# A hybrid attention and convolution layer: two latents, a row norm and the positions by other routes, the first weights in halves, one output quarter by TensorE

## The chip, the cores and the metric

The kernel runs on one core of a Trainium2 chip. The metric is the device time of one execution in microseconds (us). Five engines work side by side, each through its own list in order: TensorE (PE) multiplies matrices, VectorE (DVE) and ScalarE (ACT) work element by element, GpSimd (POOL) does small work and issues transfers, SyncE (SP) issues transfers.

## The reference, cut to what matters

x is 256 rows of 2048; w_in has 2048 x 15,424 weights; there are 16 heads.

```python
h = _rmsnorm(x, pre_norm_g)
proj = jnp.einsum('bsd,de->bse', h, w_in)
(q_a, c_kv, k_rope, z_mla, c_in, b_gate, c_gate, z_conv,
 g_mla, g_conv) = jnp.split(proj, cuts, axis=-1)
q = jnp.einsum('bsr,re->bse', _rmsnorm(q_a, q_a_norm_g), w_q_b)
...
kv = jnp.einsum('bsr,re->bse', _rmsnorm(c_kv, kv_a_norm_g), w_kv_b)
...
q_rope = _apply_rope(q_rope, cos[:, :, None, :], sin[:, :, None, :])
k_rope = _apply_rope(k_rope, cos, sin)
attn = _causal_mla_attention(q_nope, q_rope, k_nope, k_rope, v)
attn = attn.reshape(b, s, MLA_WIDTH) * jax.nn.silu(z_mla)
y_mla = jnp.einsum('bse,ed->bsd', attn, w_o_mla)
...
merged = jax.nn.sigmoid(g_mla) * y_mla + jax.nn.sigmoid(g_conv) * y_conv
out = jnp.einsum('bsd,de->bse', merged, w_out)
x = x + _rmsnorm(out, post_norm_g)
```

q_a and c_kv, the two latents, are 512 wide each; k_rope is 64 wide. cos and sin come from the positions. The row norm of x scales every row of proj.

## The kernel before, in words

**Products in two halves.** Every float32 operand is split into a rounded high half (ScalarE, line 237) and the rest (VectorE, line 238), and a product is three TensorE products: high by high, high by low, low by high. Weights come in units of 128 x 2048 values over SP's queue (load_raw, line 150), are split in halves of 1024 columns (split_unit) and are used in the order of a list, plan, that is written out by hand (lines 113 to 145). take(i) loads some units ahead and splits one ahead. There are three raw buffers, and five buffers each for the high and low halves; units 3, 4 and 5 land in areas of tiles that are not yet in use.

**Order.** Most instructions are placed by a scheduler, which takes what is ready, earlier lines first. keep_in_program_order holds a marked instruction behind those marked before it on its engine; all of TensorE's instructions are marked (lines 86 to 91).

**Start.** x comes transposed, in row blocks k of 128 features by 256 rows. The first eight units hold two such blocks each and the two matching blocks of q_a's weights. Block 0 of x comes with the small parameters (pv, line 247) on ScalarE's queue. Unit 0 comes in two pieces, units 1 and 2 in two each (line 155). Each block is scaled by pre_norm_g and split into x_both (split_scaled, line 334): block 0 is scaled by VectorE, the others by ScalarE, and VectorE makes all the low halves. Nine idle products (line 265) run on TensorE ahead of it. latent_products (line 456) accumulates q_a, with the 256 rows as two tiles; then c_kv (four units) and k_rope (u_kr) follow.

**Positions.** tables() (line 392) computes the angles on GpSimd, in a long row of small operations behind four transfers of the positions, each to 32 partitions, from GpSimd's own queue (line 396). Two sines on ScalarE follow, 32 copies into cos_t and sin_t on GpSimd (line 439) and a sign on VectorE (line 442). It is a generator: each next(table_parts) issues the part up to the next yield.

**Norms and turns.** The row norm of x is computed from x_tok: squares on ScalarE, a power on GpSimd (inverse_root, line 356), r_col by rows. input_rows (line 374) makes r_x, the same numbers along a row in every partition, by two TensorE products of ones by a diagonal (rb). latent_norm (line 465) scales a latent by rows out of PSUM into lat_f; latent_turn (line 477) transposes it with TensorE, eight transposes of 128 x 128 for each latent (lt_qa, lt_ckv), and ScalarE and VectorE make the halves, qa and ckv, from PSUM. q_a is turned after the first unit of z, c_kv in the middle of the second one (turn_keys, line 769).

**Another way to turn** stands in turned() (line 308), which the gates, the probabilities and the channels use: VectorE transposes blocks of 32 x 32 into a tile (line 312), GpSimd's queue stores it to DRAM in four transfers (go, line 319), and one load brings it back (come, line 323). A load waits for its four stores.

**First head.** z (four units) gives the gates of four heads, closed by gates_done (line 668). Then make(...) computes from qa and ckv the first group: q and k without rotation for two heads ("a": qn, kn), the rotated part of q ("r": qr, rotated by VectorE in rope, line 446) and the values ("v": vv); then a quarter of the convolution channels, channels(0, 0) (cv), and the scores of head 0 (sc, scores, line 582). sc needs qn, kn, qr and the rotated key kr (key_rope, line 523). From there, channels, scores and values alternate over 16 heads; then the wide products (sq) and the last one (out).

**End.** out_block (line 950) sums the squares of a block of 512 columns on ScalarE and multiplies by post_norm_g on VectorE. Behind the last block of a row tile, row_norm (line 961) gives rr, and finish (line 968) makes og * rr + xr on VectorE in five pieces, each stored from SP's queue.

Of the kernel before, what the change touches and what calls it, by code (L numbers as in the profile page):

```python
# [82 lines left out]
def tile_layer(ctx: ExitStack, tc: tile.TileContext, xw, x, pos, pvec, post_g, wc, wz, wcv, wkr, wqk, wqr, wv, cwr, wsq, out):  # L83
# [6 lines left out]
    def transpose(*a):  # L90
        return tc.keep_in_program_order(nc.tensor.transpose(*a))  # L91

# [69 lines left out]
    def split_unit(i):  # L162
# [84 lines left out]
    nc.scalar.dma_start(out=pv[:, :], in_=pvec)  # L247
    x_first = pv[:, -(-PV_N // LINE) * LINE :]
# [16 lines left out]
    for _ in range(9):  # L265
# [5 lines left out]
    r_both = const.tile([P, LINE], F32, name="r_both")  # L271
    r_col, r_sq = r_both[:, :NT], r_both[:, NT : 2 * NT]
# [35 lines left out]
    def turned(src, via, n):  # L308
# [4 lines left out]
        far = dram.tile([P, P * n], F32, name="far", tag=f"far{n}", bufs=4)  # L313

        def go():
            f = far[:, :].rearrange("(q y) (i m) -> i y q m", q=4, i=4)
# [4 lines left out]
        def come(dst):  # L321

            tc.keep_in_program_order(nc.gpsimd.dma_start(out=dst, in_=far[:, :]))
# [10 lines left out]
    def split_scaled(dst, src, k):  # L334
        if k == 0:
            a = nc.vector.tensor_scalar(dst[:, k, :S], src, col("pre_g", k), None, op0=ALU.mult)
        else:
            a = nc.scalar.activation(dst[:, k, :S], src, AF.Copy, scale=col("pre_g", k))
        tc.keep_in_program_order(a)
# [21 lines left out]
    def input_norm():  # L361
# [5 lines left out]
        dgs = []  # L367
        for t in range(NT):
            dg = temp(f"dg{t}", (P, P), tag=f"rms_d{t}", bufs=1)
            nc.vector.tensor_scalar(dg[:, :], ident[:, :], r_col[:, t : t + 1], None, op0=ALU.mult)  # L370
            dgs.append(dg)
        return dgs

    def input_rows(dgs):

        rb = bank("rb", tag="st", bufs=1)
        for t in range(NT):
            matmul(rb[:, t * P : (t + 1) * P], ones[:, :], dgs[t][:, :], start=True, stop=True)
        nc.scalar.activation(r_x[:, :], rb[:, :S], AF.Copy)
# [11 lines left out]

    def tables():

        pi = temp("ta_i", (P, SQ), I32, 1)
        for q in range(4):
            nc.gpsimd.dma_start(
                out=pi[32 * q : 32 * q + 32, :], in_=pos[:, SQ * q : SQ * (q + 1)].to_broadcast([32, SQ])
            )
# [36 lines left out]
        for o in range(4):  # L435
            for q in range(4):
                to, ti = slice(32 * o, 32 * o + 32), slice(32 * q, 32 * q + 32)
                for dst, src in ((cos_t, n1), (sin_t, n2)):
                    tc.keep_in_program_order(nc.gpsimd.tensor_copy(dst[to, SQ * q : SQ * (q + 1)], src[ti, :]))
        yield  # L440
# [15 lines left out]
    def latent_products(pss, k, w, wk):  # L456
        cols = [x_both[:, k, o : o + P] for o in (0, P, S, S + P)]
        wh, wl_ = w(wk, R)
        for i, ws, first, last in ((0, wh, True, False), (2, wh, False, False), (0, wl_, False, True)):
            for t in range(NT):  # L460
                matmul(
                    pss[t][:, :], cols[i + t], ws, start=first and k == 0, stop=last and k == KD - 1
                )

    def latent_norm(name, pss):
# [11 lines left out]
    def latent_turn(name, both, g, tags):  # L477
        f = lat_f[name]
        for j2 in range(2):
            ps = bank(f"lt_{name}{j2}", tag=tags[j2][0], bufs=tags[j2][1])  # L480
            for j in range(2):
                for t in range(NT):
                    o, b = j * S + t * P, 2 * j2 + j
                    transpose(ps[:, o : o + P], f[:, t, b * P : (b + 1) * P], ident[:, :])
            for j in range(2):
                b, src = 2 * j2 + j, ps[:, j * S : (j + 1) * S]
                nc.scalar.activation(both[:, b, :S], src, AF.Copy, scale=col(g, b))
                nc.vector.scalar_tensor_tensor(
                    both[:, b, S:], src, col(g, b), both[:, b, :S].bitcast(F32), op0=ALU.mult, op1=ALU.subtract
                )  # L490

    table_parts = tables()
    next(table_parts)
    ps_q = [bank(f"qa{t}") for t in range(NT)]
    for i in range(KD // 2):
        ahead(u_qa[i], raw=3 + len(early), split=0)
        w = take(u_qa[i])
        for j in range(2):
            latent_products(ps_q, 2 * i + j, w, j)
    ps_c = [bank(f"ckv{t}") for t in range(NT)]  # L500
    for i in range(4):
# [3 lines left out]
        if i == 0:  # L505
            next(table_parts)
        if i == 1:
            dg = input_norm()
            latent_norm("qa", ps_q)
# [6 lines left out]
    input_rows(dg)  # L516
    latent_norm("ckv", ps_c)
# [16 lines left out]
    def narrow(names, w, j, src, **kw):  # L534
        pss = [bank(n, **kw) for n in names]
# [117 lines left out]
    def quarter(pss, w, i, between=None):  # L653

        for t in range(NT):
            if t and between:
                between()
# [5 lines left out]
    def gates(v, i, between=None):  # L663
        if i == 0:
            z_ps["now"] = [bank(f"z{v}_{t}") for t in range(NT)]
        quarter(z_ps["now"], take(u_gate[v][i]), i, between)
# [95 lines left out]
    for h in range(H):  # L762
        v, at = divmod(h, HV)

        if at == 0:
            for i in range(4):
                if v == 0 and i == 1:

                    def turn_keys():
                        latent_turn("ckv", ckv, "kv_g", (("mm", 4), ("mm", 4)))  # L770
                        next(table_parts)

                    gates(v, i, turn_keys)
                else:
                    gates(v, i)
                if v == 0 and i == 0:
                    latent_turn("qa", qa, "q_g", (("st", 1), ("o", 1)))
                elif v == 0 and i == 2:
                    key_rope()
# [187 lines left out]

    def finish(t, rr):
        for a, b in ((0, 256), (256, 512), (512, 1024), (1024, 1536), (1536, 2048)):
# [18 lines left out]
    for t in range(NT):  # L988
# [4 lines left out]
        finish(t, out_block(3, t, pss[t]))  # L993
# [90 lines left out]
```

## Time and profile before

| | us |
|---|---|
| median of 3 runs | 1038.44 (1038.15 to 1038.61) |
| the profiled execution | 1039.19 |
| its span, first to last instruction | 1037.4 |
| TensorE busy in it | 1027.2 |

TensorE's granted clock was 0.998 of full speed. In the profile's rows "L88" is a line of the kernel; PE is TensorE's products and PEld its loading of weights; a row of the chain has a start, a length, an engine, a tile and a count. Tiles have the names that the code gives them, without numbers: qa, ckv, kr, rb, z, lt_qa, qn, kn, qr, vv, cv, sc, sq and out are banks of PSUM that TensorE writes.

### The profile page before, as it was taken

What the parts mean: (1) busy time and instruction counts of PE and PEld (TensorE: products, weight loads), DVE (VectorE), ACT (ScalarE), POOL (GpSimd) and SP (SyncE); (2) the same over time, 40 slices, a digit from 0 to 9 for tenths busy, and PEclk for the clock granted to TensorE, in tenths of its full rate; (3) what the DMA queues carried; (4) which work ended last, traced back from release to release, by engine and by line L of the source; (5) the groups of instructions that cost most, each with busy time, mean ns of one, the idle gap of its engine ahead of it and who ended that gap; (6) DMA issues with size and microseconds to landing.
All of it is one profiled execution on the core that took longest, in us unless ns stands there. A gap on an engine that the chain in (4) does not pass through costs nothing.

```text
span 1037.4 us, 12723 instructions
## 1 busy us (share of the span) xinstructions
PE 1027.2 (99%) x4694; PEld 856.3 (83%) x4694; DVE 682.3 (66%) x954; ACT 526.6 (51%) x733; POOL 181.0 (17%) x345
## 2 busy tenths in 40 slices
PE   9999999999999999999999999999999999999996
PEld 7888888888888888888888888888888888888885
DVE  7579777787687786767777785564465455455562
ACT  7767555555555455554554564444334434443551
POOL 7620321114211232212313120020010001002000
PEclk9999999999999999999999999999999999999999
DMA  8745766568565685757676766565555566558642
GB/s 323 304 175 215 232 213 234 193 222 295 190 250 202 219 282 189 272 210 243 236 262 200 261 228 212 183 228 198 203 203 209 197 203 236 181 191 331 235 165 82
DMA packets 41952, 231.04 MB, mean 223 GB/s; under 512 B 7521, under 2 KB 8225, under 8 KB 18977
## 3 DMA queue, kind: packets, MB, share of 16 engines
q1 hardware_dynamic: 29808, 197.54, 53.9%
q0 software_dynamic: 11648, 29.38, 8.5%
q10 hardware_dynamic: 432, 3.29, 0.8%
q8 instruction: 37, 0.61, 0.2%
q14 instruction: 27, 0.21, 0.1%
HBM read 214.48 MB, written 11.53 MB: 218 GB/s over the span
## 4 chain that ended last, share of the span: by engine, by line
PE 98%; DMA 1%; DVE 0%; ACT 0%; SPq 0%; DVEq 0%; issue 0%
PE cv L88 34%; PE sq L88 34%; PE z L88 8%; PE out L88 8%; PE qn L88 2%; PE kn L88 2%; PE vv L88 2%; PE ckv L88 2%; PE qa L88 2%; PE sc L88 1%; PE qr L88 1%; PE o L88 1%; DMA raw<-xw_dram 1%; PE kr L88 0%; DVE og L971 0%; PE lt_qa L91 0%
## 5 line engine op out<-in xcount | busy, mean ns | idle before, releaser
L238 DVE TENSOR_TENSOR wlo<-raw,whi 128x1024 fp32r<-128x1024 f32 (+1 forms) x370 | 441.1, 1198 | 284.1 <-ACT whi L237 273.9
L237 ACT ACTIVATE whi<-raw 128x1024 fp32r<-128x1024 f32 (+1 forms) x372 | 382.9, 1035 | 396.2 <-PE sq L88 180.5
L88 PE MATMUL cv<-whi,x_both 128*128 128x512 f32 x1024 | 321.1, 389 | 0.0
L88 PEld LDWEIGHTS cv<-whi,x_both 128*128 128x128 f32 x1024 | 192.3, 188 | 39.2
L88 PE MATMUL cv<-wlo,x_both 128*128 128x512 f32 x512 | 199.5, 390 | 0.0
L88 PE MATMUL sq<-whi,x_both 128*128 128x512 f32 x512 | 158.3, 389 | 0.0
L88 PEld LDWEIGHTS sq<-whi,x_both 128*128 128x128 f32 x512 | 96.1, 188 | 19.9
L88 PEld LDWEIGHTS cv<-wlo,x_both 128*128 128x128 f32 x512 | 96.2, 188 | 19.0
L88 PE MATMUL sq<-wlo,x_both 128*128 128x512 f32 x256 | 99.6, 389 | 0.0
L88 PE MATMUL z<-whi,x_both 128*128 128x512 f32 x256 | 80.6, 390 | 0.0
L88 PE MATMUL sq<-whi,at_both 128*128 128x512 f32 x256 | 79.5, 389 | 0.0
L88 PE MATMUL sq<-whi,cv_both 128*128 128x512 f32 x256 | 79.4, 389 | 0.0
L88 PE MATMUL out<-whi,m_both 128*128 128x512 f32 x256 | 78.9, 389 | 0.0
L319 POOL DMA_DIRECT2D far<-sg x32 | 17.5, 555 | 312.2 <-DVE sg L312 238.6
L319 POOL DMA_DIRECT2D far<-via x64 | 35.4, 560 | 195.1 <-DVE via L312 194.7
L88 PEld LDWEIGHTS sq<-wlo,x_both 128*128 128x128 f32 x256 | 48.0, 188 | 10.0
L88 PEld LDWEIGHTS z<-whi,x_both 128*128 128x128 f32 x256 | 48.1, 188 | 9.9
L88 PEld LDWEIGHTS sq<-whi,at_both 128*128 128x128 f32 x256 | 48.0, 188 | 9.9
L88 PEld LDWEIGHTS out<-whi,m_both 128*128 128x128 f32 x256 | 48.0, 188 | 9.9
L88 PEld LDWEIGHTS sq<-whi,cv_both 128*128 128x128 f32 x256 | 48.0, 188 | 9.9
L88 PE MATMUL z<-wlo,x_both 128*128 128x512 f32 x128 | 49.8, 389 | 0.0
L88 PE MATMUL sq<-wlo,at_both 128*128 128x512 f32 x128 | 49.8, 389 | 0.0
(214 smaller groups left out, 1128.0 us busy)
## 6 DMA issues: line engine op xcount, KB each, us to landing
raw<-wsq_dram SPq DMA_DIRECT2D x80, 1024.0 KB, 4.7
raw<-wcv_dram SPq DMA_DIRECT2D x64, 1024.0 KB, 5.8
raw<-wz_dram SPq DMA_DIRECT2D x16, 1024.0 KB, 4.7
raw<-wqk_dram SPq DMA_DIRECT2D x8, 1024.0 KB, 5.1
cw<-cwr_dram POOLq DMA_DIRECT2D x24, 256.0 KB, 6.2
raw<-wc_dram SPq DMA_DIRECT2D x4, 1024.0 KB, 9.9
raw<-wv_dram SPq DMA_DIRECT2D x4, 1024.0 KB, 4.7
far<-via POOLq DMA_DIRECT2D x64, 48.0 KB, 3.3
```

The costliest lines, as they stand in the source:

```text
L88: return tc.keep_in_program_order(nc.tensor.matmul(*a, **kw))
L237: a = nc.scalar.activation(hi, src, AF.Copy)
L238: b = nc.vector.tensor_tensor(lo, src, hi.bitcast(F32), op=ALU.subtract)
L319: tc.keep_in_program_order(nc.gpsimd.dma_start(out=f[i], in_=m))
```

## The change

- **Latents.** latent_norm now turns the scaled latent itself: VectorE transposes 32 x 32 blocks of each row tile, GpSimd's queue stores them (eight stores for each latent), and it hands back one load (qa_come, ckv_come). latent_split makes the halves from SBUF. TensorE's sixteen transposes go, and latent_turn and the between of quarter with them.
- **Row norm.** r_x comes by a VectorE transpose of a 128 x 32 tile, two stores and one broadcast load on GpSimd's queue. rb, its diagonals and input_rows go.
- **Positions.** The host hands them over as 128 rows; one transfer on SP's queue, behind the sixth unit, brings them. The parts of tables() are issued at other places, the copies in two parts.
- **Start.** Block 0 of x, unit 0's first weights and their splits come in halves; block 0's products too; VectorE scales block 1 as well; seven idle products for nine.
- **Order.** channels(0, 0) runs ahead of the first group, in the plan too; key_rope comes behind "a"; qr's products of the first group use the common banks.
- **End.** For the second row tile, columns 0 to 511 of the result are x by the identity plus og by a diagonal of rr on TensorE (identity product ahead of the norm), copied and stored by ScalarE; VectorE does the other 1536 in four pieces. The first row tile has four pieces.

```diff
-        order += (first if h == 0 else []) + [(h, 0), (h, 1), (h, 2)] + made[h] + [(h, 3)]
+        order += [(h, 0)] + (first if h == 0 else []) + [(h, 1), (h, 2)] + made[h] + [(h, 3)]
...
-        cuts = {0: (S, XW, 2 * XW), 1: (0, XW, 2 * XW), 2: (0, XW, 2 * XW)}.get(i, (0, w))
+        cuts = {0: (S, 2 * S, XW, 2 * XW), 1: (0, XW, 2 * XW), 2: (0, XW, 2 * XW)}.get(i, (0, w))
...
+        if i == u_qa[5]:
+            tc.keep_in_program_order(nc.sync.dma_start(out=tables_pi, in_=pos))
...
-                split_act(hi[:, j * R : (j + 1) * R], lo[:, j * R : (j + 1) * R], t[:, o + S : o + XW], True)
+                for a, b in ((0, S), (S, R)) if k == 0 else ((0, R),):
+                    cs = slice(j * R + a, j * R + b)
+                    split_act(hi[:, cs], lo[:, cs], t[:, o + S + a : o + S + b], True)
...
-    nc.scalar.dma_start(out=pv[:, :], in_=pvec)
+    for a, b in ((0, n + P), (n + P, n + S)):
+        nc.scalar.dma_start(out=pv[:, a:b], in_=pvec[:, a:b])
...
-    for _ in range(9):
+    for _ in range(7):
...
-        if k == 0:
-            a = nc.vector.tensor_scalar(dst[:, k, :S], src, col("pre_g", k), None, op0=ALU.mult)
+        if k < 2:
+
+            for a, b in ((0, P), (P, S)) if k == 0 else ((0, S),):
+                tc.keep_in_program_order(
+                    nc.vector.tensor_scalar(dst[:, k, a:b], src[:, a:b], col("pre_g", k), None, op0=ALU.mult)
+                )
...
+        rt = temp("r_turned", (P, LINE), bufs=1)
+        temp("pad_n", (P, S - LINE), bufs=1)
+        nc.vector.transpose(rt[:, :], r_both[:, :])
+        far = dram.tile([NT, S // NT], F32, name="far_r")
+        rows_of = rt[:, :].rearrange("(q y) x -> y q x", q=4)
+        for t in range(NT):
+            tc.keep_in_program_order(
+                nc.gpsimd.dma_start(out=far[t, :].rearrange("(q x) -> q x", q=4), in_=rows_of[t])
+            )
+        return lambda: tc.keep_in_program_order(
+            nc.gpsimd.dma_start(out=r_x[:, :], in_=far[:, :].rearrange("t s -> (t s)").unsqueeze(0).to_broadcast([P, S]))
+        )
...
+            for a, b in ((0, S), (S, R)) if halved else ((0, R),):
+                for t in range(NT):
+                    matmul(
+                        pss[t][:, a:b], cols[i + t], ws[:, a:b], start=first and k + a == 0, stop=last and k == KD - 1
+                    )
...
         inverse_root(r[:, :], v[:, :])
+        if then:
+            then()
         nc.vector.tensor_tensor(r[:, :], r[:, :], r_col[:, :], op=ALU.mult)
+        far = dram.tile([P, NT * R], F32, name=f"far_{name}")
         for t in range(NT):
             nc.scalar.activation(f[:, t, :], pss[t][:, :], AF.Copy, scale=r[:, t : t + 1])
+            go, _ = turned(f[:, t, :], temp("cw", (P, 512), bufs=2), 4, far[:, t * R : (t + 1) * R])
+            go()
+        return lambda: tc.keep_in_program_order(
+            nc.gpsimd.dma_start(out=f, in_=far[:, :].rearrange("p (t c) -> p t c", t=NT))
+        )
+
+    def latent_split(name, both, g):
+
+        f = lat_f[name].rearrange("p t (i k x) -> p k t i x", i=4, k=KR)
+        for k in range(KR):
+            hi, lo = (both[:, k, o : o + S].rearrange("p (t i x) -> p t i x", t=NT, i=4) for o in (0, S))
+            tc.keep_in_program_order(nc.scalar.activation(hi, f[:, k], AF.Copy, scale=col(g, k)))
+            tc.keep_in_program_order(
+                nc.vector.scalar_tensor_tensor(lo, f[:, k], col(g, k), hi.bitcast(F32), op0=ALU.mult, op1=ALU.subtract)
+            )
...
-    input_rows(dg)
-    latent_norm("ckv", ps_c)
+    r_come()
+    ckv_come = latent_norm("ckv", ps_c, qa_come)
+    next(table_parts)
+    ckv_come()
+    next(table_parts)
...
-        kw = {} if g else {"tag": "cv", "bufs": 2}
-        (f,) = narrow([f"qr{g}"], take(u_grp["r", g]), 0, qa, **kw)
+        (f,) = narrow([f"qr{g}"], take(u_grp["r", g]), 0, qa)
...
+                gates(v, i)
+                if v == 0 and i == 2:
+                    latent_split("qa", qa, "q_g")
...
+            else:
+                latent_split("ckv", ckv, "kv_g")
             gates_done(v)
         if h == 0:
+            channels(h, 0)
             for i in first:
                 make(*i)
-            channels(h, 0)
+                if i[0] == "a":
+                    next(table_parts)
+                    key_rope()
...
+    def ahead_of_norm(t):
+
+        fin = bank("fin", tag="st", bufs=1)
+        matmul(fin[:, :], ident[:, :], xr[:, t, :512], start=True, stop=False)
+        return fin
+
+    def by_tensor(t, rr, fin):
+
+        dg = op.tile([P, P], F32, name="dg_fin")
+        tc.keep_in_program_order(nc.scalar.activation(dg[:, :], ident[:, :], AF.Copy, scale=rr[:, 0:1]))
+        matmul(fin[:, :], dg[:, :], og[:, t, :512], start=False, stop=True)
+        o = op.tile([P, 512], F32, name="o_fin")
+        tc.keep_in_program_order(nc.scalar.activation(o[:, :], fin[:, :], AF.Copy))
+        nc.scalar.dma_start(out=out[t * P : (t + 1) * P, :512], in_=o[:, :])
+
     def finish(t, rr):
-        for a, b in ((0, 256), (256, 512), (512, 1024), (1024, 1536), (1536, 2048)):
+        cuts = ((0, 512), (512, 1024), (1024, 1536), (1536, 2048))
+        if t:
+            cuts = ((512, 768), (768, 1024), *cuts[2:])
```

More of the change, by code (lines that the diff above doesn't have):

```diff
@@ L271, in tile_layer @@
     r_both = const.tile([P, LINE], F32, name="r_both")
+    nc.gpsimd.memset(r_both[:, :], 0.0)
     r_col, r_sq = r_both[:, :NT], r_both[:, NT : 2 * NT]
@@ L305, in temp, with turned @@
         return bp.tile([P, -(-n // LINE) * LINE], dt, name=name, tag=tag, bufs=bufs)[:, :n]
-    def turned(src, via, n):
+    def turned(src, via, n, far=None):
         via = via[:, : P * n]
@@ L321, in come @@
         def come(dst):
-            tc.keep_in_program_order(nc.gpsimd.dma_start(out=dst, in_=far[:, :]))
+            tc.keep_in_program_order(nc.gpsimd.dma_start(out=dst, in_=far))
         return go, come
@@ L389, in rows @@
         nc.vector.tensor_tensor(dst, dst, r_x[:, :], op=ALU.mult)
+    tables_pi = temp("ta_i", (P, SQ), I32, 1)
     def tables():
[L394 to L398, printed above, removed]
+        pi = tables_pi
         y, n1, n2, r = (temp(f"ta_{n}", (P, SQ), bufs=1) for n in "ymnr")
@@ L453, in rope, with latent_products @@
         nc.vector.tensor_tensor(dst, a[:, :], b[:, :], op=ALU.add)
-    def latent_products(pss, k, w, wk):
+    def latent_products(pss, k, w, wk, halved=False):
         cols = [x_both[:, k, o : o + P] for o in (0, P, S, S + P)]
@@ L459, in latent_products, with latent_norm @@
         for i, ws, first, last in ((0, wh, True, False), (2, wh, False, False), (0, wl_, False, True)):
[L460 to L465, printed above, removed]
+            for a, b in ((0, S), (S, R)) if halved else ((0, R),):
[3 more added lines that the diff above has]
+                    )
+    def latent_norm(name, pss, then=None):
         f = lat_f[name]
@@ L532, in tile_layer, with narrow @@
     groups = {}
-    def narrow(names, w, j, src, **kw):
-        pss = [bank(n, **kw) for n in names]
+    def narrow(names, w, j, src):
+        pss = [bank(n) for n in names]
         halves([
@@ L651, in tile_layer, with quarter @@
     z_ps = {}
-    def quarter(pss, w, i, between=None):
+    def quarter(pss, w, i):
         for t in range(NT):
-            if t and between:
-                between()
             for k4 in range(4):
@@ L661, in quarter, with gates @@
                 product(pss[t][:, :], a, w(k4, 512), k == 0, k == KD - 1)
-    def gates(v, i, between=None):
+    def gates(v, i):
         if i == 0:
             z_ps["now"] = [bank(f"z{v}_{t}") for t in range(NT)]
-        quarter(z_ps["now"], take(u_gate[v][i]), i, between)
+        quarter(z_ps["now"], take(u_gate[v][i]), i)
     def gates_done(v):
@@ L992, in tile_layer @@
             out_product(pss[t], t, last[kk], kk)
-        finish(t, out_block(3, t, pss[t]))
+        fin = ahead_of_norm(t) if t else None
+        rr = out_block(3, t, pss[t])
+        if t:
+            by_tensor(t, rr, fin)
+        finish(t, rr)
 def _cols(w):
```

65 lines of the change are left out of this document (16 added, 49 removed).

## The prediction

> **What bounds the kernel now.** I read the shares of the engines first, then who TensorE (PE) waited for, then the chain of work that ended last, in order of time.
>
> ```profile
> PE 1027.2 (99%) x4694; PEld 856.3 (83%) x4694; DVE 682.3 (66%) x954; ACT 526.6 (51%) x733; POOL 181.0 (17%) x345
> ```
>
> ```profile
> PE qa L88 <- ACT whi L237: 1.2, 1, 1.2
> ```
>
> ```profile
> 1.64 6.58 DMA raw<-xw_dram
> ...
> 9.33 19.38 PE qa L88 x84
> ...
> 50.47 3.63 PE kr L88 x16
> 54.09 0.45 PE rb L88 x4
> 54.54 5.46 PE z L88 x24
> 60.00 0.87 PE lt_qa L91 x8
> 60.87 2.75 PE z L88 x12
> 63.62 0.87 PE lt_ckv L91 x8
> 64.49 13.64 PE z L88 x60
> 78.13 2.77 PE qn L88 x16
> 80.90 2.79 PE kn L88 x16
> 83.69 1.40 PE qr L88 x8
> 85.09 5.49 PE vv L88 x24
> 90.58 5.44 PE cv L88 x24
> 96.02 0.94 PE sc L88 x8
> ```
>
> The first number of a chain row is the start, the second the length, in us. TensorE is the bound: 99% busy, and behind its wait of 1.2 us, which ends at 9.33, its products follow one another to the end. So an edit counts in one of four ways: products taken out of TensorE's stream, the start of that stream, a new wait inside it, and the tail after it. What it does to the other engines costs nothing until TensorE waits for them.
>
> **The change part by part.** The profiled execution took 1039.19 us (span 1037.4 and 1.8 around it); the median of the three runs shown is 1038.44, 0.75 less. I sum differences, and apply them to both.
>
> *Products taken out.* The row norm's four instructions (rb, 0.45) and the sixteen transposes of the two latents (0.87 each) stand in the chain itself: 0.45 + 0.87 + 0.87 = **2.19 us** gone. Added there is nothing of that size: the first row block's 6 products become 12 of half the width, and the identity product of the last quarter follows TensorE's last product, in the tail.
>
> *The start.* TensorE's first real products come well before 9.33:
>
> ```profile
> 5.00 1.23 PE L88 MATMUL qa<-whi,x_both 128*128 128x512 f32 x4
> ```
>
> At the z products' pace (13.64/60 = 0.227 us) the 12 products of the first two row blocks take 2.7 us from 5.0, to 7.7; then TensorE stands until 9.33, since the third block's rows land at 1.64 + 6.58 = 8.2 and ScalarE needs 1.1 us more. Why so late? I looked at the DMA view of the first 5 us, and at stretches around it (the last column is GB/s, the one before the share of the DMA engines):
>
> ```profile
> DMA packets 508, 1.03 MB, mean 207 GB/s; under 512 B 49, under 2 KB 177, under 8 KB 508
> ```
>
> ```profile
> 5.00:8.00 3.00, 3.00 (x14) 2.17 (x13) 1.96 (x4) 1.03 (x2) 0.00 (x0) 1.00 0.88 290
> 8.00:20.00 12.00, 10.76 (x48) 8.81 (x48) 10.80 (x21) 10.96 (x24) 8.97 (x14) 1.00 1.03 429
> ```
>
> ```profile
> q0 software_dynamic: 102, 0.03, 6.5%
> ```
>
> Up to and with those rows 144 + 256 + 384 + 384 KB (by the tiles' shapes) = 1.20 MB are queued; by 5.0 us 1.03 MB had moved, so 0.17 MB were left, some 0.5 us at either stretch's rate. The rows were not whole until 8.2, and just between 5 and 8 the traffic drops from 429 to 290 GB/s. The last row is that stretch's GpSimd queue: 102 packets, of the four transfers of positions (line 396). The change takes these away: positions come on SP's queue, behind the sixth unit. So I expect the rows at some 6.2 to 6.6, ScalarE done by 7.7, and TensorE in the third block at 7.7 instead of 9.33: **1.65 us** saved. Its bounds: 0, if something else holds one DMA engine back, and 2.3, if the halved loads also bring the first two blocks 0.65 forward. I take 1.65 since the second block needs its own transfer and VectorE's chain, now one scaling longer (the scaled rows of block 1 move there from ScalarE). Two more issues, SP's and ScalarE's, stand before these rows; what matters here is queued bytes, which stay the same. Two idle products fewer only end the warm-up before the earlier start.
>
> *GpSimd's side of the positions.* On SP's queue the seventh unit's load stands behind them, and that one waits for a free buffer anyway. They land behind the sixth unit, so the angle arithmetic starts about 6.5 us later; there is a hole ahead of the row norm's power that takes it:
>
> ```profile
> 40.73 0.73 POOL L358 TENSOR_TENSOR r_both<-v_x,mhalf 128x2 f32<-128x2 f32 x1 [7.06 <-DVE v_x L364]
> ```
>
> *The latents through DRAM.* This adds four VectorE transposes, 16 stores and 2 loads on GpSimd's queue, plus 2 stores and 1 load for the row norm; 32 table copies stand around them. Their nearest rows are the gates' and probabilities' trips and the copies:
>
> ```profile
> L319 POOL DMA_DIRECT2D far<-via x28: 548/554/657, 101.8 to 287.1; - x28
> ...
> DMA to landing us min/median/max: 1.9/4.0/7.1
> ```
>
> ```profile
> L439 POOL COPY cos_t<-ta_m 32x64 f32<-32x64 f32 x16 | 8.4, 524 | 0.6
> ```
>
> The c_kv products end at 50.47 - 1.65 = 48.8. GpSimd's queue from there is, at worst in series: 8 stores of q_a (8 x 0.55 = 4.4), their landing (4.0) that q_a's load waits out, with c_kv's stores behind it, those 8 (4.4), 8 copies (4.2, beside the landing), the load (0.6 + 4.0): 70.4. VectorE's and ScalarE's norm, transposes and splits make it 75, an estimate. The q_a products are due at 79.7, c_kv's at 82.4 (z ends at 78.13 - 1.65 - 2.19 = 74.3; the first channel quarter, 5.44, now stands ahead). With 7.1 for each of three landings it is 84, 2 us too late. I take 0: the cover is z and the quarter. Key_rope's table is whole after 24 more copies (12.6), at about 78 to 82, and is due only at the first scores.
>
> *The order of the first head.* Here I see a new wait. Before, q_r's products ended at 85.09 and the first scores came at 96.02, behind the values (5.49) and a channel quarter (5.44). Now that quarter is ahead, and 5.49 plus 0.3 of score products that need no q_r are all the room. VectorE is full there:
>
> ```profile
> 82.00:96.00 14.00, 14.00 (x70) 11.79 (x69) 13.82 (x26) 9.38 (x16) 0.00 (x0) 1.00 0.42 141
> ```
>
> ```profile
> 88.49 0.42 DVE L386 TENSOR_TENSOR f<-qr,half 128x256 f32<-128x256 f32 x1
> ...
> 89.85 1.71 DVE L452 TENSOR_TENSOR rp_b<-f,sin_t 32x256 f32<-32x256 f32 x4
> ...
> 94.92 0.87 DVE L238 TENSOR_TENSOR qr<-f,qr 64x256 fp32r<-64x256 f32 x2
> ```
>
> ```profile
> L238 DVE TENSOR_TENSOR wlo<-raw,whi 128x1024 fp32r<-128x1024 f32 (+1 forms) x370 | 441.1, 1198 | 284.1 <-ACT whi L237 273.9
> ```
>
> VectorE is 13.82 of 14 us busy, and q_r's low half was done at 95.79, 10.7 after its products. Undisturbed the chain is ScalarE's half (0.4), three operations of 0.42, the four of 1.71, ScalarE's halves (0.87), VectorE's (0.87) and hand-overs: 5.6, just inside 5.8. Whatever VectorE puts between costs TensorE, as every later product is queued behind the waiting scores: one weight subtract is 1.2. The bounds are 0 and 10.7 + 3.0 - 5.8 = 7.9 (the old backlog, with key_rope's rotation, 3.0 of the same operations, fallen in between). I take one subtract, **+1.0**: moving the quarter ahead also moves VectorE's gate work and key_rope ahead of q_r, so the backlog should be smaller than it was.
>
> *The tail.* VectorE leaves the last rows' first quarter to TensorE and ScalarE:
>
> ```profile
> 1031.17 2.87 DVE L971 SCALAR_TENSOR_TENSOR og<-og,frr,xr 128x256 f32<-128x256 f32 x5
> ```
>
> ```profile
> GB/s 0 0 0 0 0 0 0 0 0 0 0 0 0 0 0 82 382 150 350 201 237 410 419 310 419 437 346 400 428 91 0 0 0 0 0 0 0 0 0 0
> ```
>
> The second row, of the DMA view, slices 1029 to 1038 us in 40. VectorE gets done about 0.7 earlier (2.87 for 2048 columns, 512 fewer), but from 1033.7 to 1035.7 the stores already run at some 400 GB/s, and the bytes are the same. I take **-0.1**; the bounds are -0.7 (VectorE set the end) and +0.5 (the new chain scale, product, copy, issue runs late). The Trainium skill says in DMA: Bandwidth & Descriptors, section Issuing engines are not separate DMA queues, that transfers issued by different engines run on the same DMA engines, so a second queue saves issue time only; by that the term would be 0 to -0.1, and the rates in the row agree.
>
> Sum: -2.19 - 1.65 - 0.1 + 1.0 = -2.9: 1036.3 in a profile, **1035.5** for the median.
>
> **The rivals.**
>
> 1. *VectorE's backlog takes over at the first scores* (slower). For it: 13.82 of 14 us, and q_r just in time before with twice the room. Against: the gate work now comes earlier, and the sin table's lateness must push key_rope into q_r's way. Full price 7.9 instead of 1.0: -3.9 + 7.9 = +4.0, 1042.4. From a wait of 3.9 nothing is left, from 6.0 the kernel is slower.
> 2. *The third block still lands late*, from a cause other than the positions. For it: only timing ties the two. Then -2.19 - 0.1 + 1.0 = -1.3: 1037.1.
> 3. *GpSimd's DMA issues are held by VectorE.* If each of the 16 stores waited out one subtract (1.2), the latents would come 19 us later, at 94 against 82.4 due: 11.6 of wait, hardly any of it shared with the scores' 1.0; -3.9 + 11.6 = +7.7, 1046.1. Against it: issues took 548 to 657 ns in 28 cases, with VectorE at work. The Trainium skill, DMA: Bandwidth & Descriptors, section SWDGE vs HWDGE vs iDMA, says that GpSimd writes its descriptors to memory that VectorE can lock it out of in a two-port mode; that speaks against this change, and the even issue times do not bear it out.
> 4. *No new wait, and the tail ends with VectorE*: -2.19 - 2.0 - 0.7 = -4.9, 1033.5.
>
> That the work isn't moved at all can be excluded: the transposes are no longer issued.
>
> **How the numbers follow.** Forecast (a wait of 0 to 2): 0.54. Rival 2: 0.13. Rival 1 in part (a wait of 2 to 6, up to 1040.5): 0.12; in full: 0.10. Rival 3: 0.03. Rival 4: 0.08. A measurement can tell about 0.2% (2.1 us) from no change: faster takes the forecast and rival 4, 0.62; same takes rival 2 and the partial rival 1, 0.25; slower the rest, 0.13. The range from 1033.4 to 1039.4 takes in rival 4, rival 2 and half of the partial waits, and leaves out what is above. The likeliest case's own range is 1034.5 to 1036.4.
>
> **What would show it.** TensorE's wait in qa gone, and the row "qa" running from about 5 without a hole: the start is right. GB/s near 400 from 5 to 8: positions were the cause. No rb and lt rows between kr and qn: 2.19. A wait of sc (or ScalarE's wait for sc moved) at about 92 of 0 to 2 us, ended by VectorE or ScalarE of q_r: the order's price. The last stores' slices still near 400 GB/s: the tail. Wrong would be a wait of qn or kn for the splits of a latent, a wait at sc above 4, or a stop at the third block as long as before.

## The result and the profile after

The changed kernel takes 1045.45 us (median of 6 runs, 1044.75 to 1046.09), the kernel before 1038.32 beside it (1038.05 to 1038.75). The ratio is 1.0069, with an interval of 1.0058 to 1.0079: slower by 7.1 us, where 1035.5 was forecast. The profiled execution took 1046.09, with a span of 1044.3: 6.9 more than that of before.

The waits of TensorE after (in total, times, longest):

```profile
PE sc L88 <- DVE qr L239: 7.0, 1, 7.0
PE fin L88 <- ACT dg_fin L984: 1.1, 1, 1.1
```

The chain that ended last, after, in order of time (start, length):

```profile
1.65 4.84 DMA raw<-xw_dram
...
7.20 20.88 PE qa L88 x90
28.07 21.76 PE ckv L88 x96
49.83 3.63 PE kr L88 x16
53.46 21.76 PE z L88 x96
75.22 5.44 PE cv L88 x24
80.66 2.77 PE qn L88 x16
...
99.81 0.43 DVE qr L239
100.23 0.04 issue
100.28 1.65 PE sc L88 x6
101.93 12.94 PE cv L88 x48
```

Read against the chain of before: c_kv's products start at 28.07 (before 9.33 + 19.38 = 28.71), so the start gave 0.64. From there to the end of z it is 47.15 us (before 49.42): 2.27 gone. z ends 2.91 early, and that is the whole gain. Then TensorE stands for 7.0 us, until VectorE has the low half of q_r. Behind the wait six score products take 1.65, and 48 channel products 12.94, where 10.91 is usual (the rows of other kernels below have it). From the end of z to the end of these 48 it is 101.93 + 12.94 - 75.22 = 39.65; before it was 29.74, which makes 9.91 more: 7.0 of wait, 2.03 in the channel products, and the other 0.88 nearly all in the scores. What follows is equal but for -0.1 in the tail. Sum: -2.91 + 9.91 - 0.1 = 6.9.

Why are products slow behind a wait? Stretches of the changed kernel: length, busy time and count of PE, PEld, DVE, ACT and POOL, then the granted clock, the share of the DMA engines and GB/s.

```profile
95.00:96.00 1.00, 0.00 (x0) 0.00 (x0) 1.00 (x3) 0.09 (x1) 0.00 (x0) 0.94 0.29 49
96.00:97.00 1.00, 0.00 (x0) 0.00 (x0) 0.99 (x3) 0.32 (x1) 0.00 (x0) 0.50 0.70 147
...
105.00:106.00 1.00, 1.00 (x4) 0.71 (x4) 0.93 (x4) 0.00 (x0) 0.00 (x0) 0.50 0.00 0
106.00:107.00 1.00, 1.00 (x6) 0.82 (x5) 0.24 (x1) 0.00 (x0) 0.46 (x1) 0.94 0.00 0
```

TensorE's clock was halved 2.6 us after it had stopped at 93.3, and stayed so until 106.1, 5.8 us after it had work again.

### The profile page after: what moved, and what is told of

The parts are those of the page before. It is cut to its first block, busy times and chain, and to the rows that moved or that the text cites. A ratio compares the mean times of both kernels' runs of the same rounds, so it can differ in the third digit from the quotient of the medians.

```text
span 1044.3 us, 12727 instructions
## 1 busy us (share of the span) xinstructions
PE 1030.3 (99%) x4680; PEld 857.6 (82%) x4680; DVE 683.6 (65%) x958; ACT 527.6 (51%) x734; POOL 186.2 (18%) x363
## 4 chain that ended last, share of the span: by engine, by line
PE 97%; DVE 1%; DMA 0%; ACT 0%; issue 0%; SPq 0%; DVEq 0%
PE cv L88 34%; PE sq L88 33%; PE out L88 8%; PE z L88 8%; PE qn L88 2%; PE ckv L88 2%; PE kn L88 2%; PE qa L88 2%; PE vv L88 2%; PE sc L88 2%; PE qr L88 1%; PE o L88 1%; DMA raw<-xw_dram 0%; PE kr L88 0%; DVE rp_b L460 0%; DVE wlo L239 0%
## 5 line engine op out<-in xcount | busy, mean ns | idle before, releaser
L239 DVE TENSOR_TENSOR wlo<-raw,whi 128x1024 fp32r<-128x1024 f32 (+2 forms) x371 | 441.4, 1195 | 292.2 <-ACT whi L238 281.6
L238 ACT ACTIVATE whi<-raw 128x1024 fp32r<-128x1024 f32 (+2 forms) x373 | 383.4, 1033 | 409.9 <-PE sq L88 180.5
```

The source lines that it names most:

```text
L238: a = nc.scalar.activation(hi, src, AF.Copy)
L239: b = nc.vector.tensor_tensor(lo, src, hi.bitcast(F32), op=ALU.subtract)
```

## Where VectorE's time went

Two stretches, from the end of z (0.6 to 0.7 us before it) to the end of q_r's low half: first before, then after.

```profile
77.50:95.80 18.30, 18.30 (x91) 15.50 (x90) 18.09 (x30) 13.44 (x22) 0.00 (x0) 1.00 0.48 172
```

```profile
74.50:100.70 26.20, 19.20 (x96) 16.21 (x95) 24.20 (x44) 15.73 (x29) 4.00 (x14) 0.91 0.61 216
```

The third busy time and count are VectorE's: 18.09 us of work in 30 instructions before, 24.20 in 44 after, and 2.0 of idle time in place of 0.2. The stretch is 7.9 longer: 7.0 of that is the wait, the rest comes of where the two stretches are cut and of two score products that run ahead of the wait. What the 14 more are, VectorE's order of time shows:

```profile
79.02 1.62 DVE L502 SCALAR_TENSOR_TENSOR ckv<-at_f,pv,ckv 128x256 fp32r<-128x256 f32 x4
...
90.67 0.35 DVE L450 TENSOR_SCALAR sin_t<-sin_t,pv 128x256 f32<-128x256 f32 x1
...
91.97 1.71 DVE L460 TENSOR_TENSOR rp_b<-at_f,sin_t 32x256 f32<-32x256 f32 x4
```

c_kv's low halves (1.62) and the key's rotation (0.42 + 0.35 + 1.71 + 0.42 + 0.42 = 3.32), all of which VectorE did under z before: 4 and 8 instructions. The other two are subtracts of weights of half width (0.69 each). Both are late on GpSimd's queue. c_kv's share of it, after:

```profile
49.94 4.43 POOL L324 DMA_DIRECT2D far_qa<-cw  x8 [5.17 <-DVE cw L316]
56.85 0.58 POOL L386 DMA_DIRECT2D r_x<-far_r  x1 [2.49 <-DMA far_qa<-cw]
57.45 0.89 POOL L366 TENSOR_TENSOR r_ckv<-v_ckv,mhalf 128x2 f32<-128x2 f32 x1
58.31 0.59 POOL L492 DMA_DIRECT2D at_f<-far_qa  x1
63.16 4.35 POOL L324 DMA_DIRECT2D far_ckv<-cw  x8 [4.26 <-DVE cw L316]
70.53 0.56 POOL L492 DMA_DIRECT2D at_f<-far_ckv  x1 [0.92 <-ACT whi L238]
```

The brackets are idle times of GpSimd: 5.2 until VectorE has transposed q_a, 2.5 until stores have landed, 4.3 until VectorE has transposed c_kv. ScalarE takes c_kv up at 76.99. Before, the low halves were done at about 67. The table's last copy ends at 78.8.

## The experiments

The kernel before ran beside each group; its medians were 1038.2 to 1038.4. In the first four expectations theory A is that VectorE's order makes the wait, B is its rival. The other letters are explained where they first stand; G is a rival in b1, and another idea, the theory, in r1 and s1.

**e1: the key's rotation ahead of the first group.**

```diff
         if h == 0:
             channels(h, 0)
+            next(table_parts)
+            key_rope()
             for i in first:
                 make(*i)
-                if i[0] == "a":
-                    next(table_parts)
-                    key_rope()
```

> The changed kernel, with the table's sign and the key's rotation issued ahead of the first group instead of behind its keys. Theory A (VectorE's order: the sign is pinned behind the keys' low half, so the key's rotation of 3 us stands in front of q_r's and the first scores wait 7.0 us; the pause then halves TensorE's clock for 2.9 us more): the wait falls to 2 to 4 us, the slow stretch shrinks with it, 1038 to 1042 us. Theory B (the latents' trip through DRAM is what comes late and pushes everything on VectorE back): the wait stays within 1 us of 7.0 and the time within 1 us of 1045.5.

1045.45, ratio 1.0066 (1.0051 to 1.0081). The rotation ran from 87.7 instead of 92.0; the wait was 6.2 instead of 7.0. A falls and B's forecast came: what is moved ahead pushes the rest back, since VectorE is full.

**e2: 28 idle products ahead of the first scores.**

```diff
+            idle2 = bank("idle2", tag="o", bufs=1)
+            for _ in range(28):
+                matmul(idle2[:, :P], ones[:, :], ones[:, :], start=True, stop=True)
```

> The changed kernel, with 28 idle products (about 6.3 us at full clock) on TensorE behind the values of the first group, so that it works through most of the wait. If the products after the wait run at half pace because of the pause (granted clock 0.50 from 100 to 106 us), they now run at full pace and the time falls by about 2.9 us, to 1042.5, with the scores at the same 100.3. If they were slow for another reason (operands late), it stays at 1045.5.

1042.89, ratio 1.0045 (1.003 to 1.006). The chain of this kernel:

```profile
100.08 0.98 PE sc L88 x6
101.06 10.91 PE cv L88 x48
```

The scores start when they did (100.28 after), but all behind them runs at full pace: 2.6 us less. The slow clock's price is shown, and the rest of the loss is the wait.

**e3: the first head's order of before.**

```diff
-        order += [(h, 0)] + (first if h == 0 else []) + [(h, 1), (h, 2)] + made[h] + [(h, 3)]
+        order += (first if h == 0 else []) + [(h, 0), (h, 1), (h, 2)] + made[h] + [(h, 3)]
...
-            channels(h, 0)
...
+            channels(h, 0)
```

> The changed kernel with the first head's order undone: group ahead of the first channel quarter, q_r's first products in the channels' banks; all the rest stays. Theory A: q_r has 10.9 us of room again, no wait at the scores beyond 1 us; the keys are due at 78.0 and c_kv's low halves were done at 80.6, so a wait of up to 2.7 at kn: 1036 to 1039 us. Theory B: the wait goes to kn with 5 us or more: 1041 us and up.

1046.11, ratio 1.0075 (1.006 to 1.0091). The waits of this kernel:

```profile
PE kn L88 <- DVE ckv L502: 3.9, 1, 3.9
PE sc L88 <- DVE qr L239: 2.8, 1, 2.8
```

The moved quarter alone is not the cause. Without it the wait stands in two places, 6.7 in all, and the first of them names c_kv's low halves. A's 1036 to 1039 was missed; the time is in B's range, though the wait at kn is 3.9 and not 5 or more.

**e4: q_r first, then the quarter, then "a" and "v".**

```diff
         if h == 0:
+            next(table_parts)
+            key_rope()
+            make("r", 0)
             channels(h, 0)
-            for i in first:
-                make(*i)
...
+            make("a", 0)
+            make("v", 0)
```

> The changed kernel with another order of the first head: sign and key's rotation, then q_r's products, the channel quarter, the group's q and k, the values, the scores. Theory A: q_r has 16 us of room, c_kv stays covered, no wait over 1 us anywhere and no slow clock: 1045.5 - 9.9 = 1035.6 us. Theory B: the wait stays at 5 us or more at kn or at the scores, 1042 us and up.

1041.67, ratio 1.0035 (1.0021 to 1.0049). Two waits again, 3.2 at vv and 2.1 at sc, 5.3 in all. Neither theory had it right: A's 1035.6 was missed, B's 1042 just missed, and the order alone left most of the wait.

**g1: both latents by TensorE and the first head's order of before; the other parts kept.** In this run and in b1 the parts of tables() stand where they stood in the kernel before.

```diff
-            go, _ = turned(f[:, t, :], temp("cw", (P, 512), bufs=2), 4, far[:, t * R : (t + 1) * R])
-            go()
+                    transpose(ps[:, o : o + P], f[:, t, b * P : (b + 1) * P], ident[:, :])
```

> The change without its largest part: positions by row, first weights in halves, row norm through DRAM and the last quarter stay; the two latents are turned by TensorE again, and the channel quarter stands behind the first head's products, as before. Theory C (the latents' way through GpSimd's one queue brings c_kv some 10 us later, so VectorE does under the first head what it did under z, and has no room there): no wait of kn, and none of sc above 1 us; the clock stays at 0.998; time = before - 0.64 (start) - 0.45 (rb) - 0.1 (tail) + 0 to 0.6 = 1037.0 to 1037.7. Rival D (positions on SP's queue or the row norm through DRAM hold GpSimd and VectorE up by themselves): a wait of some us at the first scores stays, 1041 or more.

1041.71, ratio 1.0033 (1.0021 to 1.0046). No wait of kn or sc, as theory C has it, but a new one of 1.9, of ckv, explained by b1. C's time, 1037.0 to 1037.7, was missed, and rival D's 1041 or more came: positions on SP's queue do hold TensorE up, though not at the scores. Since latents, order and the places of the table's parts change together here, g1 alone does not show which of them took the wait of sc away.

**g2: positions on GpSimd's queue again; g3: that, and c_kv's power ahead of r_x's load.**

```diff
-        if i == u_qa[5]:
-            tc.keep_in_program_order(nc.sync.dma_start(out=tables_pi, in_=pos))
...
-    r_come()
-    ckv_come = latent_norm("ckv", ps_c, qa_come)
+    ckv_come = latent_norm("ckv", ps_c, lambda: (r_come(), qa_come()))
```

> The change with one part undone: the positions come on GpSimd's queue again, at the start; all else as in the changed kernel. Theory C: the angle arithmetic ends 6.5 us earlier, but GpSimd's next step, the row norm's power, waits for x as before, so c_kv still comes at about 77; wait at sc 6 to 7, slow clock behind it, the third block late again by about 0.6: 1045 to 1046.5. Rival E (the positions' lateness is what makes GpSimd late): c_kv 5 us earlier, wait at sc below 3, 1041 or less.

> As the one before (positions on GpSimd's queue at the start), and c_kv's power stands ahead of the load of the turned row norm in GpSimd's queue, so that it no longer waits for that load's turn. Theory C: c_kv's powers 3 us earlier, its load lands at about 74, its low halves are done in VectorE's idle time before z ends; the wait at sc shrinks by 1 to 3 us and the clock may stay up: 1041 to 1044.5. Rival F (c_kv's arrival doesn't matter, VectorE's whole load up to q_r's low half does, with four transposes more and 2.9 us less room): the wait stays above 6, 1045 or more.

1045.54 (ratio 1.007, 1.0055 to 1.0085) and 1045.67 (1.0069, 1.0054 to 1.0084). The wait was 7.0 in both. g2 went as expected. g3's edit did not do what it was for: the power came at 54.86 instead of 57.45, but VectorE's next step of that norm stands behind two subtracts in VectorE's list, and c_kv's low halves began at 79.49. It tells nothing for or against F.

**b1: the kernel before with the positions by row on SP's queue.**

```diff
+        if i == u_qa[5]:
+            tc.keep_in_program_order(nc.sync.dma_start(out=tables_pi, in_=pos))
```

> The kernel before with one part of the change: positions by row on SP's queue behind the sixth unit, nothing else. Theory C: no packets of GpSimd's queue between 5 and 8 us, the third block's rows whole at about 6.8 to 7.3 instead of 8.2, TensorE's c_kv products start 0.9 to 1.6 us earlier than 28.71, and at most 0.5 of it is lost at the first scores: 1036.6 to 1037.6. Rival G (the first loads' time doesn't hang on the positions, and the changed kernel's 0.64 came of the halves): 1038.0 to 1038.4.

1042.19, ratio 1.0036 (1.0023 to 1.0049). The start came as forecast, 27.06 by TensorE's order of time, against 28.55 before by the same view. But C's time, 1036.6 to 1037.6, was missed, since then TensorE waited; the waits, and ScalarE's and VectorE's order of time in this kernel:

```profile
PE ckv L88 <- ACT whi L239: 2.4, 1, 2.4
```

```profile
38.80 0.26 ACT L431 ACTIVATE ta_n<-ta_r 128x64 f32<-128x64 f32 x1 [10.06 <-DVE ta_r L429]
```

```profile
38.57 0.20 DVE L429 TENSOR_SCALAR ta_r<-ta_r 128x64 f32<-128x64 f32 x1 [9.65 <-POOL ta_r L405]
```

The angles began 5.9 us later than before (15.80 against 9.93), the clamp came 4.9 later (38.57 against 33.71), and the clamp and the sines, held in program order, kept VectorE and ScalarE for 10 us from the next weights. The change itself has these steps three units later.

**p1: b1 with the table's parts where the change has them; p2: that with the row norm through DRAM and the last quarter by TensorE; p3: that with q_a through DRAM, c_kv by TensorE one z unit later.**

```diff
-        if i == 0:
+        if i == 3:
             next(table_parts)
...
+    next(table_parts)
     latent_norm("ckv", ps_c)
+    next(table_parts)
...
-            latent_norm("qa", ps_q)
+            qa_come = latent_far("qa", ps_q)
```

> The kernel before with the positions by row on SP's queue, and the steps of the cos and sin tables that ScalarE and VectorE do moved behind the last c_kv unit, as in the changed kernel (8 copies ahead of c_kv's power, 24 behind it, the sign ahead of the key's rotation under z). In the run with the positions alone TensorE's c_kv products began 1.49 us earlier (27.06 against 28.55) and then lost 2.4 us to a wait for ScalarE, held by the clamp, and some more to a slow clock. If that is the whole of it: start kept, no wait of ckv, none of sc above 0.5: 1036.7 to 1037.3. Rival: the table is now so late that the key's rotation falls behind z, as in the changed kernel: a wait of 1 to 3 us at sc, 1038 or more.

> The one before it with the row norm turned through DRAM (0.45 of products gone) and the last quarter by TensorE (-0.1): 0.5 less than that one, 1036.2 to 1036.8, if GpSimd's two stores and one load more hold nothing up. Rival: the load's wait for the stores' landing delays c_kv's power and so its turn under z: a wait of z or sc of 1 us or more, and nothing gained.

> The one before it with one latent, q_a, through DRAM as in the changed kernel, and c_kv turned by TensorE, one z unit later than before; the first head's order is that of before. Theory C (the cost of the change is c_kv's lateness and what it pushes behind z; q_a has room): 0.87 less than the one before it, wait at sc at most 0.5: 1035.3 to 1036.0. Theory F (each latent's trip loads VectorE with 1.3 us of transposes and delays the table on GpSimd's queue, and VectorE has no room): a wait of 1.5 to 3 us at sc, 1037 or more.

p1: 1037.82, ratio 0.9996 (0.9987 to 1.0005); p2: 1037.54, 0.9993 (0.9984 to 1.0003); p3: 1042.19, 1.0034 (1.0021 to 1.0048). p1 and p2 have no wait in TensorE's stream, but miss their forecasts of 1036.7 to 1037.3 and 1036.2 to 1036.8. p1's c_kv products start at 27.18, p2's and p3's at 27.79 and 27.86, though all three load alike. p3 waits:

```profile
PE sc L88 <- DVE qr L240: 2.6, 1, 2.6
...
PE kn L88 <- DVE at_f L709: 0.7, 1, 0.7
```

c_kv's halves were under z here, but the table's copies, behind q_a's stores and their landing on GpSimd's queue, ended at 70.7, and the key's rotation fell behind z. C's number was missed and F's came. F holds two things, the transposes on VectorE and the table's delay; the last two runs part them.

**b2: the halves alone, with block 1 by VectorE and seven idle products.**

```diff
-        cuts = {0: (S, XW, 2 * XW), 1:
+        cuts = {0: (S, 2 * S, XW, 2 * XW), 1:
...
-    nc.scalar.dma_start(out=pv[:, :], in_=pvec)
+    for a, b in ((0, n + P), (n + P, n + S)):
+        nc.scalar.dma_start(out=pv[:, a:b], in_=pvec[:, a:b])
```

> The kernel before with one part: the first unit's first weights and x in halves, block 1 scaled by VectorE, seven idle products. If the smaller rows slow the first loads (218 GB/s between 3 and 5 us in the changed kernel, 398 before): the first product at some 4.15 instead of 5.0, but the third block no earlier or later, c_kv's products begin 0 to 0.6 us later than 28.55: 1038.2 to 1038.9. Rival (the halves gain and the slow start had another cause): 0.65 earlier, 1037.6.

1038.58, ratio 1.0002 (0.9993 to 1.0012): no difference that can be told, as forecast. Its c_kv products begin at 28.08 by TensorE's order of time, where 28.55 to 29.15 was forecast and 27.9 by the rival. Its stretch from 3 to 5 us, and p1's, which loads in whole pieces:

```profile
3.00:5.00 2.00, 2.00 (x11) 2.00 (x11) 1.43 (x5) 0.98 (x3) 2.00 (x6) 1.00 0.92 229
```

```profile
3.00:5.00 2.00, 2.00 (x12) 2.00 (x11) 0.75 (x2) 0.63 (x1) 0.00 (x0) 1.00 1.02 372
```

**r1: the changed kernel with the table put right; s1: p3 with the same.** Positions behind the second unit, all 32 copies ahead of q_a's stores, sign and rotation under z. In s1 c_kv's power also stands ahead of the two loads; c_kv's low halves begin at 67.75 there and at 67.84 in p3, so that this changed nothing that counts.

```diff
-        if i == u_qa[5]:
+        if i == u_qa[1]:
...
-            if o == 0:
+            if o == 1:
                 yield
...
-            qa_come = latent_norm("qa", ps_q)
+            qa_come = latent_norm("qa", ps_q, lambda: next(table_parts))
...
+                if v == 0 and i == 1:
+                    next(table_parts)
+                    key_rope()
```

> The changed kernel with one thing put right: the cos and sin tables. The positions come on SP's queue behind the second unit instead of the sixth, half of GpSimd's 32 copies stand ahead of the row norm's power and half behind q_a's, all ahead of q_a's stores, and the sign and the key's rotation stand under z again. Both latents still go through DRAM, c_kv comes as late as before, and the first head's order is that of the change. Theory G (TensorE waits at the first scores for VectorE work that the late latents and the late table push behind z: c_kv's low halves 1.6, the key's rotation 3.3, some 1.5 of subtracts and 1.4 of idle time beside them): the rotation goes back under z, the wait falls from 7.0 to 3 to 4 us, the slow clock shrinks with it, c_kv alone keeps the rest: 1039.5 to 1042.5. Rival (the four transposes and the whole of VectorE's load decide, wherever the rotation stands): the wait stays above 5.5, 1044 or more.

> The run with q_a alone through DRAM, with the table put right in the same way, and c_kv's power ahead of the two loads. Theory G: neither c_kv nor the key's rotation is behind z, so no wait of sc or kn above 0.5 is left, and the 0.87 us of q_a's transposes are gained: 1036.3 to 1037.2. Rival (VectorE's two transposes more for q_a and the room lost decide): a wait of 1.5 to 3 us at sc stays, 1039 or more.

r1: 1042.24, ratio 1.0039 (1.0023 to 1.0054). s1: 1036.5 (11 runs), ratio 0.9983 (0.9974 to 0.9992). r1's wait, and the stretches of r1 and of s1 that answer to those of before and after:

```profile
PE sc L88 <- DVE qr L239: 3.8, 1, 3.8
```

```profile
74.60:97.50 22.90, 19.09 (x95) 16.12 (x94) 21.20 (x36) 15.12 (x27) 0.00 (x0) 0.97 0.55 200
```

```profile
75.20:93.50 18.30, 18.30 (x91) 15.49 (x90) 18.10 (x30) 13.43 (x22) 0.00 (x0) 1.00 0.55 203
```

With the rotation back under z VectorE has 21.20 us in 36 instructions and the wait falls from 7.0 to 3.8. r1 differs from the changed kernel in the table alone, so 3.2 of the wait are the table's. s1 has 18.10 in 30, what VectorE had before, and no wait of sc or kn, though VectorE still does q_a's transposes: the chain of s1 runs from 5.34 to the scores without a hole.

```profile
5.34 22.43 PE qa L88 x96
27.77 21.76 PE ckv L88 x96
...
75.84 2.77 PE qn L88 x16
...
93.73 0.94 PE sc L88 x8
94.67 10.91 PE cv L88 x48
```

Both forecasts of theory G came: late arrivals push VectorE's work behind z, and there it costs. F's other half falls for q_a: two transposes more cost nothing while they lie under z. For c_kv's two it was not tried, and what r1's 3.8 is made of stays open in part. s1 has not only c_kv by TensorE but also the first head's order of before and whole first pieces. The 3.1 us that VectorE has more in r1's stretch are c_kv's low halves (1.63) and two subtracts of half width (0.68 and 0.69), which s1 does outside it; what share of these subtracts the moved quarter has, no run shows. That c_kv's halves alone are late enough is shown by e3, where kn waits 3.9 for them. s1 beats both kernels, by 0.17% and by about 0.9%.

## Why the prediction was wrong, point by point

- **The step that failed** is in *The latents through DRAM*: "I take 0: the cover is z and the quarter", and "Key_rope's table ... is due only at the first scores". It asked whether c_kv's products would be in time, and they were: no wait of qn or kn. It put at nothing what this work of VectorE does to q_r, which comes behind it: c_kv's low halves are counted only in the time at which c_kv is ready, the key's rotation (3.0) only in the upper bound of the next term and in rival 1. c_kv's halves were done at 80.6 and the table at 78.8, inside the estimates (75 to 84, 78 to 82); the 1.6 and 3.3 us of VectorE work that they bring then stood in a stretch that the prediction itself had shown full, 13.82 of 14. r1 prices the table at 3.2 us of wait. The 3.8 that are left are gone in s1, with c_kv in time and the order of before; e3 has 3.9 for c_kv alone.
- **The order of the first head**: "I take one subtract, +1.0", since "the backlog should be smaller". It was 7.0, between the bounds, near rival 1's 7.9, and above the 4 that the prediction named as the sign of being wrong. Rival 1 was the right place and nearly the right price. But with the quarter moved back (e3) 6.7 of wait remained, so the moved quarter, which the prediction put into it, is not the cause by itself.
- **The clock** was in no term and in no rival: 2.9 us in the profile, 2.6 by e2. Rival 1 with it makes 1042.4 + 2.9 = 1045.3, close to what was measured, but partly by luck: its wait is 0.9 too long and its start 1.0 too good.
- **Products taken out**: 2.19 forecast, 2.27 found.
- **The start**: 1.65 forecast, 0.64 found. The cause was right: by TensorE's order of time the first c_kv product comes at 28.08 to 28.55 in the four traces with positions on GpSimd's queue (before, b2, g2, g3), at 27.02 to 27.92 in the twelve without. The size was not. The working lets TensorE stand from 7.7 to 9.33, but the wait of 1.2 that it shows begins at 8.1. And it hung on one execution: that of before, 1039.19, lies above the 65 other runs of that kernel on record (1037.63 to 1039.1), so that the 1.49 and 1.53 by which b1 and p1 start earlier in the profile are more than the medians bear out: p1 gains 0.39. That the profiled run was late at its third block is argued, since there is no other trace of before. The halves may eat a part: without positions on GpSimd's queue the first c_kv product comes at 27.29 to 27.92 with them (seven traces) and at 27.02 to 27.70 with whole pieces (five). The two overlap, so this is not shown.
- **The tail**: -0.1 forecast and found. The last stores' slices, after:

```profile
GB/s 0 0 0 0 0 0 0 0 0 0 0 0 0 0 0 86 378 150 360 191 237 410 419 310 428 428 391 382 410 82 0 0 0 0 0 0 0 0 0 0
```

  They differ from those of before by at most 45 GB/s (slices of 1036 to 1045 us).
- **Rivals 2 to 4**: rival 2 was right in part. ScalarE took the third block up when its rows had landed, at 7.66 instead of 8.25, and its products began at 8.74 instead of 9.33; that is 0.6 of the 1.65. (The 4.84 in the chain, to 6.5, is the second block's piece.) ScalarE's order of time, after:

```profile
7.66 0.51 ACT L347 ACTIVATE x_both<-raw,pv 128x256 fp32r<-128x256 f32 x1 [0.52 <-DMA raw<-xw_dram]
```

  Issues of the new stores took 4.43/8 = 0.55 and 4.35/8 = 0.54 us beside a busy VectorE, against rival 3. A wait came, against rival 4.
- In words: the section on the kernel before says that a marked instruction stays behind those marked before it. It stays behind what is written before it on its engine, marked or not. The sign is written behind the keys' low half, which is not marked and ran at 90.00; so the sign came at 90.67, although the last copy had ended at 78.8.

## What to carry to other kernels

When a result is made to arrive later, ask not only whether its reader's reader is in time, but which engine has work to do on arrival, and whether that engine is full there. Work that is moved from an idle stretch of VectorE into a full one cost about its whole length here (3.3 us of sign and rotation, 3.2 of wait), on the engine that waits next. And a term that is read from one execution should be held against the spread of the runs before it is added to a median.

## What the runs showed of the hardware

- **The slow clock lasted 3.4 us or a multiple of it.** The granted clock was 0.50 for 3.4 us in p3 (97.8 to 101.2), b1 (41.6 to 45.0), g1 (41.7 to 45.1), e4 (91.7 to 95.1) and twice in e3, for 6.8 in r1 (96.0 to 102.8) and g2 (99.0 to 105.8), and for 10.2 after (95.9 to 106.1) and in e1 (95.7 to 106.0). The ends in p3:

```profile
97.00:98.00 1.00, 0.13 (x1) 0.13 (x1) 0.94 (x3) 0.63 (x2) 0.00 (x0) 0.88 0.67 156
...
101.00:102.00 1.00, 1.00 (x5) 0.83 (x4) 0.38 (x3) 0.69 (x4) 0.00 (x0) 0.91 1.01 426
```

  The Trainium skill says in TensorE: Matmul & The Clock Gate, section Part 1: The HAM clock gate (the "warmup" mystery), that the array falls to half its clock after an idle window of about 3.4 us, and gets it back after a window of that length of sustained work. The trace agrees on the half and on lengths near one, two and three such windows. It differs on the pause that is needed: 2.6 us in p3, 2.4 in b1 and 1.9 in g1 were enough. Nor does the pause's length decide alone: 2.1 in e4 left the clock at 1.00, and behind the same pause of 7.0 the clock was slow for 10.2 us in the changed kernel and for 6.8 in g2. g1's wait, and the stretch of e4 that holds the pause of 2.1:

```profile
PE ckv L88 <- ACT whi L241: 1.9, 1, 1.9
```

```profile
98.00:102.00 4.00, 1.94 (x13) 1.78 (x13) 3.92 (x9) 2.59 (x7) 0.00 (x0) 1.00 0.29 70
```

- **Halved first pieces went with slower first loads.** The first loads of 128 rows, the first pieces cut to half as many bytes a row, moved 171 to 257 GB/s between 3 and 5 us in the ten kernels that have them (218 after, 229 in b2); whole ones moved 372 (p1) to 398 (before) in the other six. That it is the shorter rows that do it is argued.
